# Building a scan's phase tables on GpSimd, and one rotation of eight PSUM banks for an FFN

## The chip, the core and the metric

One core of a Trainium2 chip runs the whole program. The metric is device time in microseconds (us) from launch to end. The engines are TensorE (PE; its weight loads are shown apart as PEld), VectorE (DVE), ScalarE (ACT), GpSimd (POOL) and SyncE (SP), which here only issues DMAs. Each engine works through its own queue in order and waits on semaphores for the others.

## The reference, cut to what matters

One layer of a diffusion backbone over 2048 latent tokens with 1024 channels and 256 context tokens, in float32:

```
n      = modulate(rmsnorm(x))                      # latent and context
q,k,v,u,gates = split(n @ w_in)
a      = neighbourhood_attention(rope(q), rope(k), v, context keys, bias)
s      = s5_branch(u)      # per group and state p: h[t] = lam[p]*h[t-1] + B u[t], lam complex,
                           # forward and backward, y = Re(C h) + D u, gelu, GLU
h      = x + g1 * ((sig(ga)*(a@w_ba) + sig(gs)*(s@w_bs)) @ w_out)
f      = modulate(rmsnorm(h))
h      = h + g2 * ((silu(f@W1) * (f@W2)) @ w_ffn_out)       # hidden 2816
out    = rmsnorm(h) * g
```

## The kernel before

Every matmul operand is split into a rounded high part and a remainder (`split`, L68: ACT writes `whi`, L70, then DVE writes `wlo`, L71), and each product is three matmuls. Weights come through SP's DMAs in pieces (`raw`, `piece`) and pass two short buffer rotations, `wr` (raw) and `wh` (split pairs; four pairs in the FFN).

A scheduling compiler orders the instructions of each engine. It goes by the order of the program, by priorities set in the code and by its own estimate of each instruction's time. `hot()` raises the priority of a few instructions, above all evacuations of PSUM. `run` (L1203) gives the scan and then the attention the high priority. The input projection (`in_proj`) stands 100000 lower and fills what they leave free, and the merge another 100000 lower.

**The scan** (`s5`, L629). Tokens are taken in chunks of 8, so that the scan runs over 288 chunk columns (32 of context, 256 latent). Eight sub-blocks are made (four `q`, two `sb` each), and each has two pairs of groups and two directions, so 32 rounds in all (L729 to L773). A round needs a table of the phases exp(i*theta*t) for 288 columns, real part `er` and imaginary part `ei`. It is built by doubling: 32 columns are copied from `eb`, then four levels (m = 32, 64, 128, 256; widths 32, 64, 128, 32) each multiply what is there by a complex constant from `zz`. ACT makes the copies (L734, L735) and one product of each part (L741, L742), DVE the two others with the sums (L743, L744). Then PE makes `pv` (L750), DVE rotates it with the table (L757 to L760), runs the scan instruction (L762), rotates back (L765, L766) and writes the states `hs` (L771, L772). `er` and `ei` have two buffers, `ea` and `eb` one. POOL issues the loads of `ut` (L651) for the scan. In the same stretch it builds the attention's bias tables (`biases`, L430): for each of 8 heads a load (L436), four additions (L442, L443) and three stores (L445), through the same ring of 12 buffers from which `in_proj` takes its `n` tiles.

While scan and projection run, only two PSUM banks (pool `gpm`) belong to the projection. Its evacuations are by DVE (L384 and what follows) and ACT (L382, L412, L426).

**The FFN** (`ffn`, L1096) goes through four blocks of 512 tokens; each has three groups of hidden tiles. For every hidden tile pair `ffn_in` (L1019) is called twice. It is one step of a fast 2x2 block multiplication: seven products (`prod`, L1063) of 12 matmuls with 256 columns (L1067 to L1069), in place of eight. Its weight sums are made by POOL (L1036 to L1050), and four pieces are split in the order s13, s24, (a11, a22), a12. The products share two PSUM banks, each as two halves: `pa` and `pb`.

| product, in order | writes | read by |
|---|---|---|
| s1 | pb half 1 | ACT copy to v, L1076 |
| s3 | pb half 0 | DVE add into v, L1079 |
| s2 | pa half 1 | DVE add into u, L1085 |
| s4 | adds to pb half 1 | DVE, L1087 |
| a11 | pa half 0 | ACT copy to u, L1084 |
| a22 | adds to pb half 0 | DVE, L1090 |
| a12 | adds to pa half 0 | ACT copy, L1093 |

Within one bank a write by PE and a read by another engine are kept apart by semaphores, also where the halves differ. The tiles `ps` come from a pool of four banks, so two calls fit. Behind a group's calls the output product runs (L92 to L94 with `po`): for both halves `c` of the channels, four token tiles each hold one bank of another pool of four (`fpo`) through all hidden tiles of the group, and are then added to `acc`. In a block's last group the next block's normalized input `X` is prepared between the weight pieces (`norm_ffn`, L990), in four steps that take two `ps` banks each.

Of the kernel before, what the change touches and what calls it, by code (L numbers as in the profile page):

```python
# [10 lines left out]
F32 = mybir.dt.float32  # L11
F32R = mybir.dt.float32r
BF16 = mybir.dt.bfloat16
AF = mybir.ActivationFunctionType
ALU = mybir.AluOpType
PSUM = bass.MemoryType.PSUM
DRAM = bass.MemoryType.DRAM

P = 128
# [33 lines left out]
class Kernel:  # L53
# [575 lines left out]
    def s5(self):  # L629
        nc, I = self.nc, self.I  # L630
        V = nc.vector
        with ExitStack() as ctx:
# [7 lines left out]
            for q in range(4):  # L640
                yn = [bp.tile([P, SC, 8, 16], F32, name=f"yn{cb}") for cb in range(2)]
                for sb in range(4 // NQ):
# [84 lines left out]
                    for p0 in range(0, NQ, 2):  # L727
                        hst = {}
                        for p in (p0, p0 + 1):  # L729
                            for d in range(2):  # L730
                                pr = d * 16 + pr0 + p
                                er = pp.tile([P, SEQC], F32, name="er")
                                ei = pp.tile([P, SEQC], F32, name="ei")
                                nc.scalar.copy(er[:, 0:32], self.eb[:, 0, :, pr])  # L734
                                nc.scalar.copy(ei[:, 0:32], self.eb[:, 1, :, pr])  # L735
                                for i, m in enumerate((32, 64, 128, 256)):
                                    w = min(m, SEQC - m)
                                    zr, zi, zn = (self.zz[:, i, x, pr:pr + 1] for x in range(3))
                                    ea = pp.tile([P, P], F32, name="ea", bufs=1)
                                    eb = pp.tile([P, P], F32, name="eb", bufs=1)  # L740
                                    nc.scalar.activation(ea[:, :w], er[:, 0:w], AF.Copy, scale=zr)  # L741
                                    nc.scalar.activation(eb[:, :w], ei[:, 0:w], AF.Copy, scale=zr)  # L742
                                    V.scalar_tensor_tensor(er[:, m:m + w], ei[:, 0:w], zn, ea[:, :w], op0=ALU.mult, op1=ALU.add)  # L743
                                    V.scalar_tensor_tensor(ei[:, m:m + w], er[:, 0:w], zi, eb[:, :w], op0=ALU.mult, op1=ALU.add)  # L744
# [274 lines left out]
    def ffn_in(self, ch, b, X, pm, os, tp, up):  # L1019
# [40 lines left out]
        pa = pm.tile([P, 2, 256], F32, name="ps")  # L1060
        pb = pm.tile([P, 2, 256], F32, name="ps")

        def prod(dst, a, x, first=True):  # L1063
            for k in range(4):
                mm = nc.tensor.matmul
                xh, xl = X[k][:, 0, x], X[k][:, 1, x]
                mm(dst, a[0][:, k], xh, start=(first and k == 0), stop=False, skip_group_check=True)  # L1067
                mm(dst, a[0][:, k], xl, start=False, stop=False, skip_group_check=True)  # L1068
                mm(dst, a[1][:, k], xh, start=False, stop=(k == 3), skip_group_check=True)  # L1069
# [4 lines left out]
        prod(pb[:, 1], s1, 3)  # L1074
        with self.hot():
            nc.scalar.copy(v, pb[:, 1])  # L1076
        prod(pb[:, 0], s3, 5, False)
        with self.hot():
            V.tensor_tensor(v, pb[:, 0], v, op=ALU.add)  # L1079
        prod(pa[:, 1], s2, 4)  # L1080
        prod(pb[:, 1], s4, 2, False)
        prod(pa[:, 0], a11, 0, False)
        with self.hot():
            nc.scalar.copy(u, pa[:, 0])  # L1084
            V.tensor_tensor(u, pa[:, 1], u, op=ALU.add)  # L1085
            V.tensor_tensor(c[1][:, 1], u, v, op=ALU.add)
            V.tensor_tensor(c[0][:, 1], pb[:, 1], u, op=ALU.add)  # L1087
        prod(pb[:, 0], a22, 6, False)
        with self.hot():
            V.tensor_tensor(c[1][:, 0], pb[:, 0], u, op=ALU.add)  # L1090
        prod(pa[:, 0], a12, 1, False)
        with self.hot():
            nc.scalar.copy(c[0][:, 0], pa[:, 0])  # L1093
        return [x.rearrange("p a t -> p (a t)") for x in c]

    def ffn(self, xs_, os, xp, tp, pm, first):  # L1096
        nc, I = self.nc, self.I
        V = nc.vector
        with ExitStack() as ctx:
# [5 lines left out]
            up = self.pool("fu", 2, ctx)  # L1105
# [3 lines left out]
            po = self.pool("fpo", 4, ctx, space=PSUM)  # L1109
# [3 lines left out]
            for b in range(NB):  # L1113
# [4 lines left out]
                for g, (p0, p1) in enumerate(groups):  # L1118
# [45 lines left out]
                    for c in range(2):  # L1164
                        cs = slice(c * 512, c * 512 + 512)
                        pos = {j: po.tile([P, 512], F32, name="po") for j in range(4)}
# [178 lines left out]
```

## Time and profile before

| | us |
|---|---|
| median of 3 runs | 3296.73 |
| lowest and highest run | 3295.64, 3303.11 |
| the profiled execution's own time | 3294.7 |
| its span, first to last instruction | 3292.9 |
| PE busy | 3140.3 (95%) |
| PEld busy | 2738.5 (83%) |
| DVE busy | 2313.2 (70%) |
| ACT busy | 1598.6 (49%) |
| POOL busy | 882.4 (27%) |

All views are of one profiled execution. Busy time counts instructions at work. A matmul is shown longer than the distance to the next one, since matmuls are pipelined, so a busy PE is not a PE at its peak. A wait of an engine is shown with the instruction that ended it. The mean granted clock of TensorE was 0.983 of full speed.

### The profile page before, as it was taken

The numbers are of one execution on the slowest core, as the hardware profiler recorded it, in microseconds if no ns is written. First come the engines' busy times: TensorE is split into PE (matmuls) and PEld (weight loads), VectorE is DVE, ScalarE is ACT, GpSimd is POOL, SyncE is SP. The second block draws the span as 40 slices with busy tenths as digits, with TensorE's granted clock in tenths as the row PEclk, the third lists the DMA queues.
The fourth block names the chain that finished last, engine by engine and source line by source line (L and its number), as shares of the span: only waits on it lengthen the run. The fifth ranks groups of instructions, "written<-read, shape, count | busy, mean of one in ns | idle before, by whom it ended". The sixth has DMA issues, their size and how long they took to land.

```text
span 3292.9 us, 54200 instructions
## 1 busy us (share of the span) xinstructions
PE 3140.3 (95%) x20600; PEld 2738.5 (83%) x20600; DVE 2313.2 (70%) x4121; ACT 1598.6 (49%) x2778; POOL 882.4 (27%) x856
## 2 busy tenths in 40 slices
PE   8999978999899999899999999999999999999998
PEld 6987766777788778778898888889989898989988
DVE  6688787888353475565657766887869856886666
ACT  4455434554465545456553444444535543554534
POOL 2000052001232222223200444632241423442242
PEclk9999989999999999999999999999999999999999
DMA  8445566445776887786847334434344333343332
GB/s 333 171 122 168 170 203 221 164 140 165 231 210 189 243 267 231 225 261 191 259 145 243 131 129 137 138 128 144 113 139 146 121 116 130 134 149 130 107 112 100
DMA packets 212852, 564.27 MB, mean 171 GB/s; under 512 B 31784, under 2 KB 63656, under 8 KB 212592
## 3 DMA queue, kind: packets, MB, share of 16 engines
q1 hardware_dynamic: 155008, 437.48, 40.1%
q0 software_dynamic: 28032, 87.64, 9.8%
q10 hardware_dynamic: 29552, 35.70, 3.2%
q8 instruction: 162, 2.65, 0.3%
q14 instruction: 98, 0.80, 0.1%
HBM read 446.95 MB, written 111.61 MB: 170 GB/s over the span
## 4 chain that ended last, share of the span: by engine, by line
PE 72%; DVE 11%; DMA 9%; issue 3%; ACT 2%; POOL 2%; SPq 0%; ACTq 0%; DVEq 0%; POOLq 0%
PE ps L92 10%; PE ps L94 10%; PE ps L93 10%; PE ps L1067 6%; PE ps L1069 6%; PE ps L1068 6%; PE po L93 4%; PE po L92 4%; PE po L94 4%; DVE wlo L71 4%; PE o L924 3%; DMA raw<-in_w_m 2%; DMA n<-in_rpb 2%; PE w L884 2%; PE w L905 1%
## 5 line engine op out<-in xcount | busy, mean ns | idle before, releaser
L71 DVE TENSOR_TENSOR wlo<-raw,whi 128x1024 fp32r<-128x1024 f32 (+1 forms) x522 | 661.5, 1269 | 350.1 <-ACT whi L70 341.3
L70 ACT CAST whi<-raw 128x1024 fp32r<-128x1024 f32 (+1 forms) x522 | 507.6, 974 | 536.0 <-PE ps L1068 141.5
L1067 PE MATMUL ps<-X,whi 128*128 128x256 f32 x2464 | 700.0, 285 | 30.8 <-DVE u L1085 10.6
L1069 PE MATMUL ps<-X,wlo 128*128 128x256 f32 x2464 | 689.9, 285 | 10.0 <-DVE wlo L71 8.6
L1068 PE MATMUL ps<-X,whi 128*128 128x256 f32 x2464 | 694.4, 283 | 0.0
L1067 PEld LDWEIGHTS ps<-X,whi 128*128 128x128 f32 x2464 | 471.7, 191 | 42.2 <-DVE u L1085 16.2
L1069 PEld LDWEIGHTS ps<-X,wlo 128*128 128x128 f32 x2464 | 465.8, 191 | 17.9 <-DVE wlo L71 17.9
L1068 PEld LDWEIGHTS ps<-X,whi 128*128 128x128 f32 x2464 | 471.8, 191 | 1.3
L92 PE MATMUL ps<-n,whi 128*128 128x512 f32 (+1 forms) x800 | 321.5, 402 | 32.0 <-DVE t L384 17.6
L93 PE MATMUL ps<-n,whi 128*128 128x512 f32 (+1 forms) x800 | 318.4, 398 | 0.0
L94 PE MATMUL ps<-n,wlo 128*128 128x512 f32 (+1 forms) x800 | 317.5, 398 | 0.0
L93 PE MATMUL po<-wlo,zh 128*128 128x512 f32 x704 | 277.6, 394 | 0.0
L94 PE MATMUL po<-whi,zl 128*128 128x512 f32 x704 | 275.6, 394 | 0.0
L92 PE MATMUL po<-whi,zh 128*128 128x512 f32 x704 | 270.4, 394 | 0.0
L92 PEld LDWEIGHTS ps<-n,whi 128*128 128x128 f32 x800 | 152.6, 191 | 73.0 <-DVE t L384 14.7
L1049 POOL TENSOR_TENSOR os<-raw 128x512 f32<-128x512 f32 x66 | 96.2, 1457 | 391.6 <-DMA raw<-in_w_f 364.2
L1050 POOL TENSOR_TENSOR os<-raw,os 128x512 f32<-128x512 f32 x88 | 147.0, 1670 | 190.4 <-DMA raw<-in_w_f 188.2
L71 DVE TENSOR_TENSOR wlo<-os,whi 128x1024 fp32r<-128x1024 f32 x110 | 149.2, 1356 | 60.8 <-ACT whi L70 60.6
L70 ACT CAST whi<-os 128x1024 fp32r<-128x1024 f32 x110 | 115.3, 1048 | 143.8 <-POOL os L1050 41.9
L94 PEld LDWEIGHTS ps<-n,wlo 128*128 128x128 f32 x800 | 152.7, 191 | 36.3 <-issue 3.5
L93 PEld LDWEIGHTS ps<-n,whi 128*128 128x128 f32 x800 | 153.1, 191 | 33.7 <-issue 2.1
L92 PE MATMUL ps<-y,whi 128*128 128x512 f32 x384 | 157.1, 410 | 10.4 <-DVE t L968 5.1
(341 smaller groups left out, 7101.7 us busy)
## 6 DMA issues: line engine op xcount, KB each, us to landing
raw<-in_w_f SPq DMA_DIRECT2D x198, 512.0 KB
raw<-sums SPq DMA_DIRECT2D x66, 512.0 KB
raw<-in_w_gate SPq DMA_DIRECT2D x64, 512.0 KB
raw<-in_w_f SPq DMA_DIRECT2D x66, 256.0 KB
raw<-in_w_qk SPq DMA_DIRECT2D x32, 512.0 KB
gsc<-e ACTq DMA_DIRECT2D x64, 256.0 KB
raw<-in_w_m SPq DMA_DIRECT2D x32, 512.0 KB
t<-gsc SPq DMA_DIRECT2D x64, 256.0 KB
```

Of the source, the lines that this page charges most:

```text
L70: self.nc.scalar.copy(hi, x)
L71: self.nc.vector.tensor_tensor(lo, x, hi.bitcast(F32), op=ALU.subtract)
L92: mm(ps, l[0], r[0], start=first, stop=False)
L93: mm(ps, l[0], r[1], start=False, stop=False)
L94: mm(ps, l[1], r[0], start=False, stop=last)
L884: nc.tensor.matmul(slv, q[:, qs], kl, start=(n == 0), stop=(n == 1))
L924: nc.tensor.matmul(o[h, g, :, hf, :], l, r, start=(n == 0), stop=(n == nb + 1), skip_group_check=True)
L1049: nc.gpsimd.tensor_tensor(s24[:, 0], s13[:, 0], a11, op=ALU.subtract)
L1050: nc.gpsimd.tensor_tensor(s24[:, 1], a12, s24[:, 0], op=ALU.subtract)
L1067: mm(dst, a[0][:, k], xh, start=(first and k == 0), stop=False, skip_group_check=True)
L1068: mm(dst, a[0][:, k], xl, start=False, stop=False, skip_group_check=True)
L1069: mm(dst, a[1][:, k], xh, start=False, stop=(k == 3), skip_group_check=True)
```

## The change

In the scan, the real and the imaginary part of a table stand in one tile `ee` with two halves, and POOL alone builds it. One copy takes both parts of the first 32 columns. Each level is four instructions: both parts by the real constant, both parts by the imaginary constant into `ea`, then a subtraction for the real part and an addition for the imaginary part. A round thus has 17 POOL instructions in place of 10 on ACT and 8 on DVE. `er`/`ei` keep two buffers and `ea` one; `eb` falls away.

In the FFN, each call of `ffn_in` takes four banks and uses one half of each. The order of the products becomes s1, s3, a11, s2, s4, a22, a12, and `u` gets a third buffer. The pool `fpo` joins the `ps` pool in one rotation of eight banks, which also serves the output product and `norm_ffn`.

```
-  er = pp.tile([P, SEQC], F32, name="er")
-  ei = pp.tile([P, SEQC], F32, name="ei")
-  nc.scalar.copy(er[:, 0:32], self.eb[:, 0, :, pr])
-  nc.scalar.copy(ei[:, 0:32], self.eb[:, 1, :, pr])
+  ee = pp.tile([P, 2, SEQC], F32, name="er")
+  er, ei = ee[:, 0], ee[:, 1]
+  G = nc.gpsimd
+  G.tensor_copy(ee[:, :, 0:32], self.eb[:, :, :, pr])
   for i, m in enumerate((32, 64, 128, 256)):
       w = min(m, SEQC - m)
-      zr, zi, zn = (self.zz[:, i, x, pr:pr + 1] for x in range(3))
-      ea = pp.tile([P, P], F32, name="ea", bufs=1)
-      eb = pp.tile([P, P], F32, name="eb", bufs=1)
-      nc.scalar.activation(ea[:, :w], er[:, 0:w], AF.Copy, scale=zr)
-      nc.scalar.activation(eb[:, :w], ei[:, 0:w], AF.Copy, scale=zr)
-      V.scalar_tensor_tensor(er[:, m:m + w], ei[:, 0:w], zn, ea[:, :w], op0=ALU.mult, op1=ALU.add)
-      V.scalar_tensor_tensor(ei[:, m:m + w], er[:, 0:w], zi, eb[:, :w], op0=ALU.mult, op1=ALU.add)
+      zr, zi = (self.zz[:, i, x, pr:pr + 1].unsqueeze(1).to_broadcast([P, 2, w]) for x in range(2))
+      ea = pp.tile([P, 2, P], F32, name="ea", bufs=1)
+      G.tensor_tensor(ee[:, :, m:m + w], ee[:, :, 0:w], zr, op=ALU.mult)
+      G.tensor_tensor(ea[:, :, :w], ee[:, :, 0:w], zi, op=ALU.mult)
+      G.tensor_tensor(er[:, m:m + w], er[:, m:m + w], ea[:, 1, :w], op=ALU.subtract)
+      G.tensor_tensor(ei[:, m:m + w], ei[:, m:m + w], ea[:, 0, :w], op=ALU.add)
...
-  pa = pm.tile([P, 2, 256], F32, name="ps")
-  pb = pm.tile([P, 2, 256], F32, name="ps")
+  pb1, pb0, pa1, pa0 = (pm.tile([P, 2, 256], F32, name="ps")[:, 0] for _ in range(4))
...
-  prod(pb[:, 1], s1, 3)
+  prod(pb1, s1, 3)
   with self.hot():
-      nc.scalar.copy(v, pb[:, 1])
-  prod(pb[:, 0], s3, 5, False)
+      nc.scalar.copy(v, pb1)
+  prod(pb0, s3, 5)
   with self.hot():
-      V.tensor_tensor(v, pb[:, 0], v, op=ALU.add)
-  prod(pa[:, 1], s2, 4)
-  prod(pb[:, 1], s4, 2, False)
-  prod(pa[:, 0], a11, 0, False)
+      V.tensor_tensor(v, pb0, v, op=ALU.add)
+  prod(pa0, a11, 0)
   with self.hot():
-      nc.scalar.copy(u, pa[:, 0])
-      V.tensor_tensor(u, pa[:, 1], u, op=ALU.add)
+      nc.scalar.copy(u, pa0)
+  prod(pa1, s2, 4)
+  with self.hot():
+      V.tensor_tensor(u, pa1, u, op=ALU.add)
       V.tensor_tensor(c[1][:, 1], u, v, op=ALU.add)
-      V.tensor_tensor(c[0][:, 1], pb[:, 1], u, op=ALU.add)
-  prod(pb[:, 0], a22, 6, False)
+  prod(pb1, s4, 2, False)
   with self.hot():
-      V.tensor_tensor(c[1][:, 0], pb[:, 0], u, op=ALU.add)
-  prod(pa[:, 0], a12, 1, False)
+      V.tensor_tensor(c[0][:, 1], pb1, u, op=ALU.add)
+  prod(pb0, a22, 6, False)
   with self.hot():
-      nc.scalar.copy(c[0][:, 0], pa[:, 0])
+      V.tensor_tensor(c[1][:, 0], pb0, u, op=ALU.add)
+  prod(pa0, a12, 1, False)
+  with self.hot():
+      nc.scalar.copy(c[0][:, 0], pa0)
...
-  up = self.pool("fu", 2, ctx)
+  up = self.pool("fu", 3, ctx)
-  po = self.pool("fpo", 4, ctx, space=PSUM)
+  pm = Rotation(pm, 4, self.pool("fpo", 4, ctx, space=PSUM), 4)
-  pos = {j: po.tile([P, 512], F32, name="po") for j in range(4)}
+  pos = {j: pm.tile([P, 2, 256], F32, name="ps").rearrange("p a t -> p (a t)") for j in range(4)}
```

## Rows read from the trace of the kernel before

**Rows 1.** Busy time in stretches: scan, its bias part, FFN; us of each engine, clock, DMA.
```profile
165.00:825.00 660.00, 618.41 (x3432) 494.68 (x3431) 547.94 (x1113) 320.69 (x678) 89.33 (x104) 0.97 0.54 169
400.00:545.00 145.00, 112.97 (x615) 92.23 (x614) 115.70 (x189) 62.44 (x122) 63.03 (x66) 0.89 0.67 213
...
1822.00:3293.00 1471.00, 1421.87 (x9682) 1310.16 (x9681) 1095.19 (x1408) 689.12 (x1052) 541.34 (x355) 0.99 0.38 128
```

**Rows 2.** Waits of PE in the whole span: us in total, times, longest us.
```profile
PE ps L92 <- DVE t L384: 18.8, 8, 6.4
...
PE ps L92 <- ACT e L412: 10.9, 1, 10.9
PE ps L1067 <- DVE u L1085: 10.6, 11, 3.2
PE ps L1067 <- DVE u L1079: 10.5, 11, 1.6
...
PE ps L1069 <- DVE wlo L71: 8.6, 13, 1.9
...
PE ps L1067 <- ACT u L1076: 3.8, 2, 2.1
...
PE ps L1067 <- DVE n L1087: 2.8, 3, 1.6
```

**Rows 3.** Timeline of PE in the FFN: start us, us, engine, line, idle before.
```profile
2109.40 0.28 PE L1069 MATMUL ps<-X,wlo 128*128 128x256 f32 x1
2110.93 0.39 PE L1067 MATMUL ps<-X,whi 128*128 128x256 f32 x1 [1.25 <-DVE u L1079]
...
2577.09 0.39 PE L1067 MATMUL ps<-X,whi 128*128 128x256 f32 x1 [2.06 <-ACT u L1076]
2577.32 0.28 PE L1068 MATMUL ps<-X,whi 128*128 128x256 f32 x1
2577.43 0.29 PE L1069 MATMUL ps<-X,wlo 128*128 128x256 f32 x1
```

**Rows 4.** Timeline of DVE in the first of those two stretches.
```profile
2108.77 1.77 DVE L71 TENSOR_TENSOR wlo<-raw,whi 128x512 fp32r<-128x512 f32 x1
2110.47 0.41 DVE L1079 TENSOR_TENSOR u<-ps,u 128x256 f32<-128x256 f32 x1
```

**Rows 5.** The chain that ended last, 2095 to 2122 us (FFN, first block), by line.
```profile
by line: DVE wlo L71 20.8%; DVE n L1129 18.1%; PE ps L1067 13.0%; PE ps L1068 11.0%; PE ps L1069 10.4%; issue 7.8%; DVE n L1126 5.1%; DVE zl L71 4.5%; DVE n L1090 4.0%; ACT whi L70 3.9%; DVE u L1079 2.5%; DVE u L1085 1.3%; ACTq L70 0.1%; DV
```

**Rows 6.** Groups by line, the table's instructions: count, busy us, mean ns, idle before.
```profile
L741 ACT ACTIVATE ea<-er,zz 128x32 f32<-128x32 f32 (+2 forms) x128 | 44.2, 345 | 62.8 <-DVE er L743 61.7 <-DVE ei L744 0.4 <-issue 0.3
...
L742 ACT ACTIVATE eb<-ei,zz 128x32 f32<-128x32 f32 (+2 forms) x128 | 43.5, 340 | 26.9 <-DVE ei L744 21.0 <-DMA ks<-qt 2.8 <-DMA vs<-e 2.6
...
L743 DVE SCALAR_TENSOR_TENSOR er<-ei,zz,ea 128x32 f32<-128x32 f32 (+2 forms) x128 | 38.0, 297 | 3.4 <-ACT ea L741 2.5
...
L744 DVE SCALAR_TENSOR_TENSOR ei<-er,zz,eb 128x32 f32<-128x32 f32 (+2 forms) x128 | 37.7, 294 | 2.9 <-ACT eb L742 2.7
```

**Rows 7.** Timeline of DVE through scan rounds of one sub-block.
```profile
359.62 0.76 DVE L757 TENSOR_TENSOR p<-pv,er 128x576 f32<-128x576 f32 x1 [0.79 <-PE pv L750]
...
363.86 0.68 DVE L766 TENSOR_TENSOR p<-v,ei 128x512 f32<-128x512 f32 x1
...
365.89 0.42 DVE L772 TENSOR_TENSOR h<-p,p 64x256 f32<-64x256 f32 x1
...
377.13 0.76 DVE L757 TENSOR_TENSOR p<-pv,er 128x576 f32<-128x576 f32 x1
```

**Rows 8.** Groups by line on POOL, each shape apart; columns as in rows 6.
```profile
L442 POOL TENSOR_TENSOR n<-am,n 128x480 f32<-128x480 f32 x16 | 20.5, 1302 | 69.1 <-DMA n<-in_rpb 54.2 <-issue 14.9
L443 POOL TENSOR_TENSOR n<-n,am 128x480 f32<-128x480 f32 x16 | 18.6, 1168 | 0.2
...
L140 POOL MEMSET mhalf<- 128x4 f32 x1 | 0.1, 98 | 0.0
```

**Rows 9.** Waits of POOL in 165 to 825 us; columns as in rows 2.
```profile
POOL n L442 <- DMA n<-in_rpb: 54.2, 7, 10.0
```

**Rows 10.** Groups by line on DVE, 165 to 405 us (POOL nearly idle).
```profile
L71 DVE TENSOR_TENSOR wlo<-raw,whi 128x1024 fp32r<-128x1024 f32 x28 | 34.1, 1217 | 12.1 <-ACT whi L70 11.9
```

**Rows 11.** The same, 405 to 525 us (POOL at the bias tables).
```profile
L71 DVE TENSOR_TENSOR wlo<-raw,whi 128x1024 fp32r<-128x1024 f32 x12 | 17.2, 1431 | 5.2 <-ACT whi L70 5.2
```

## The prediction

> **What bounds the kernel now.** I read the page's engine shares first, then busy time by stretch, then who PE waited for, then timelines where those waits lie. PE is busy 95% of the span in the table of times. By stretch it is 618 of 660 us in the scan (0.97 of its clock) and 1422 of 1471 us in the FFN, where the next engine, DVE, has 1095; in the scan DVE has 548 of 660, ACT 321 and POOL 89 [rows 1]. So the time is PE's work plus PE's waits. The change leaves the matmuls as they are, so its worth is PE waits that go or come. DVE, ACT and POOL time counts only where it makes PE wait. The reader should see in [rows 2] that few waits are long enough to matter: for the scan stretch the projection's evacuation, L384 (18.8 us) and L412 (10.9); for the FFN the readers of the shared product banks and the weight split (8.6). And the weak spot in [rows 1]: in 400 to 545, where POOL makes the bias tables, PE has 113 of 145 us and a clock of 0.89.
>
> **FFN, what is removed.** Four rows of [rows 2] are PE waiting to write one half of a bank while the other half is read: L1085 10.6, L1079 10.5, L1076 3.8, L1087 2.8, together 27.7 us in 27 waits. A waiting matmul's predecessor is shown 0.28 us long although the next starts 0.11 to 0.12 us behind it where nothing waits (2577.32 to 2577.43) [rows 3], so each wait is understated by some 0.16 us: 27 x 0.16 = 4.3, in all 32.0 us. One of them, read closely: PE stands from 2109.40 to 2110.93 for L1079, which could not start before 2110.47 because a weight split of 1.77 us was ahead of it on DVE [rows 3, 4]. PE did not need that number; it needed the bank. With four banks per call, s3 no longer waits for the copy of s1, a22 no longer for the reads of s4's half, a12 no longer for L1085; s4 comes two products later and in a bank whose copy was taken four products before. All four waits lose their cause.
>
> **FFN, what comes back.** PE then runs on until something else is late, and next is the weight split, on the same DVE. In the first block DVE already sets the pace: in 2095 to 2122 wlo, L1129, L1126, zl and the evacuations L1090, L1079, L1085 make 56.3% of the chain, the matmuls 34.4% [rows 5]. The L1079 waits that I looked up lie mostly in that block, so I give back half of them, 5 us. The order is also less kind to weights: a11 is third instead of fifth, so its piece must be split two products earlier, while its buffer is still freed by the sixth product of the call before. And norm_ffn's eight bank requests now share the rotation with the output product: the third and fourth pair get banks that the first channel half holds until it has been added up. Eight is a whole turn, so the two calls of a pair still get different fours. For these two I give back 3 us; nothing, if the scheduler finds other products to put first, and up to 24 more if every removed wait turns into one for wlo. So the FFN gives 32 - 5 - 3 = **24 us**, bounds 0 and 32.
>
> **Scan, what is removed.** DVE loses L743 and L744, 38.0 + 37.7 = 75.7 us, and ACT L741 and L742, 44.2 + 43.5 = 87.7 us, and its copies [rows 6]. ACT is far from full there [rows 1], so its part is worth nothing by itself; the cover is PE's projection work.
>
> **Scan, what is added.** A table is 16 two-input instructions and a copy on POOL. Elements per partition: copy 64; products 2 x (64 + 128 + 256 + 64) = 1024; sums 2 x (32 + 64 + 128 + 32) = 512; in all 1600. The trace has no POOL instruction of these shapes. Nearest rows: L443, 480 elements with a broadcast operand, 1.17 us, and a memset of 4 elements, 0.098 us [rows 8]. If the time grows with the elements, that is 0.098 + 2.23 ns each, and a table costs 17 x 0.098 + 1600 x 0.00223 = 5.2 us. If every one cost a whole L443, 16 x 1.17 = 18.7 us. I take 5.2, since seven of ten elements are in instructions of 128 to 256 elements, between the two rows: 32 x 5.2 = 168 us of POOL, in a stretch where it had 89 of 660 [rows 1].
>
> Does the scan wait for it? A buffer is given back when L766 of two rounds before ends (364.5), and the round that uses it next starts L757 at 377.1, 12.6 us later; DVE's own work for a round runs from 359.6 to 366.3, 6.7 us [rows 7]. A POOL table of 5.2 us is inside both. So the rounds go no slower, rather a little faster, and PE's projection fills whatever they leave; of the L384 waits [rows 2] I take 3 us off, those outside the bias part being the smaller half.
>
> POOL and DVE disturb each other. The same weight split takes 1.217 us while POOL is nearly idle and 1.431 us, 18% more, while POOL makes bias tables [rows 10, 11]. POOL's additions there are 16 x 1.302 + 16 x 1.168 = 39.5 us of 120, 33% [rows 8]. At 168 us of about 645, 26%, I estimate 14% on DVE instructions. On the 472 us that DVE keeps in the scan (548 - 76) that is up to 66 us, which nearly eats the 75.7. Hence no more than the 3 us.
>
> The Trainium skill says the same in "SBUF — State Buffer", section "Who interferes with whom": a DVE instruction with two SBUF inputs contends with a GpSimd instruction that reads SBUF. The trace agrees with its 18%. The Trainium skill's "GPSIMD Engine Reference", section 4.1, advises against two-input elementwise work on GpSimd as about two times slower than on VectorE; no run so far has this table on POOL.
>
> **The bias part** is where POOL's order costs. L442 waits there 54.2 us in 7 waits for its load, 7.7 each, at most 10.0 [rows 9]; what stands behind it in POOL's queue waits too. Some four rounds fall in these 120 us. If their table instructions lie behind such a wait, L757 waits on DVE, behind it the projection's evacuations, and PE with its two banks. Bounds: nothing, if the tables fall into POOL's idle gaps; 4 x 7.7 = 31 us of waiting plus 4 x 5.2 = 21 us by which the bias chain is stretched, together 52. I take 7, near the lower end, since two tables are made ahead and a 5.2 us table fits a 7.7 us gap, which the scheduler may or may not use.
>
> **Sum**, on the profiled execution: 3294.7 - 24 (FFN) - 3 (scan rounds) + 7 (bias part) = 3274.7. That execution lies 2.0 us under the median of the runs, so the median should be 3276.7, **3277 us**, 0.6% faster. About 0.2%, 6.6 us, is what a measurement of this kernel can tell from no change.
>
> **Rivals.**
> - *The bias part holds up the scan* (the other side). One mechanism: tables queued on POOL behind L442's waits. For it: PE already loses 32 of 145 us there [rows 1], and POOL's queue is strictly in order. Against it: POOL idles between the heads. It gives +45 in place of +7: 3296.7 - 24 - 3 + 45 = 3315. It turns the sign beyond 27 + 6.6 = 34 us, four tables that each wait a whole load.
> - *The weight split takes over in the FFN.* For it: DVE's share of the chain [rows 5] and 8.6 us of wlo waits already there [rows 2]. Against it: the FFN's DVE is at 1095 of 1471 [rows 1]. The FFN gives 8: 3296.7 - 8 + 4 = 3293, no change to be told. If the joined rotation brought nothing else than new waits between the output product and the calls, it would look the same.
> - *POOL's tables are slow*, 18.7 us each with the slowing of DVE. Two buffers then give a table every (18.7 + 6.7) / 2 = 12.7 us, where the two rounds from 359.6 to 377.1 in [rows 7] took 8.8 each. 32 x 3.9 = 125 us later on DVE; PE has projection work for most of it, and I charge a fifth, 25: 3296.7 - 24 + 7 + 25 = 3305. This is what the Trainium skill's "GPSIMD Engine Reference", section 4.1, advises against.
> - *More than forecast.* All 32 us of the FFN come home and 15 of the 29.7 us of L384 and L412 [rows 2] go, because DVE and ACT answer sooner: 3296.7 - 32 - 15 = 3250.
>
> **How the numbers follow.** Chances: forecast 0.48, bias part 0.17, weight split 0.15, slow tables 0.08, more 0.12. The range reaches from the last case to the slow tables and part of the bias case: 3252 to 3306. That leaves about half of "more" below it and 0.1 above. The forecast's own range is 3266 to 3288. Faster by over 0.2%: 0.46 of the forecast, 0.12, a third of the weight case and a little of the bias case, 0.65. Within 0.2%: 0.02, half of the weight case and a fifth of the others, 0.14. Slower: the rest, 0.21.
>
> **What would show it.** PE's waits for L1079, L1085, L1076, L1087 (at their new lines) gone or under 5 us, and those for wlo not above 17: FFN right. POOL's table instructions of 0.17 to 0.67 us, 5 to 7 us a table, and L757 waiting for POOL hardly at all: scan right. L757 waiting on POOL for tens of us in the bias part, or PE busy under 105 us in its 145: the first rival. The prediction fails if the reordering by the scheduler moves loads or evacuations elsewhere, above all in the attention, which I count as unchanged.

## The result, and the profile after

| | before | after |
|---|---|---|
| median of 4 runs, us | 3296.8 | 3248.9 |
| lowest and highest run | 3295.6, 3303.1 | 3246.7, 3249.9 |
| span of the profiled execution | 3292.9 | 3247.2 |
| first product of the FFN starts (timeline of PE) | 1831.5 | 1817.7 |
| last matmul ends | 3284.6 | 3238.2 |

The ratio is 0.985, 95% interval 0.9833 to 0.9867: 48 us faster, outside the predicted range of 3252 to 3306 by 3 us and 28 us below the predicted value of 3277. From the last two rows, 13.8 us of it lie ahead of the FFN and 32.6 in the FFN (1453.1 to 1420.5).

Busy time by stretch, after; it answers to [rows 1]:

```profile
165.00:825.00 660.00, 627.23 (x3451) 498.09 (x3450) 540.35 (x851) 236.06 (x357) 381.24 (x641) 0.98 0.53 167
400.00:545.00 145.00, 125.82 (x673) 102.02 (x672) 109.01 (x147) 49.22 (x74) 91.90 (x123) 0.93 0.73 225
1822.00:3247.00 1425.00, 1391.62 (x9568) 1290.39 (x9566) 1101.87 (x1401) 677.75 (x1038) 545.49 (x350) 1.00 0.39 131
```

In the scan, POOL went from 89 to 381 us, ACT from 321 to 236. DVE lost table instructions that add up to 75.7 us [rows 6], but its busy time only fell from 548 to 540: much of what it kept got longer. In the bias part, where the prediction feared a loss, PE gained 13 us.

Waits of PE in the whole span, after; they answer to [rows 2]:

```profile
PE ps L92 <- DVE t L384: 13.6, 7, 5.1
PE w L904 <- ACT s L897: 12.4, 4, 6.7
PE ps L1067 <- DVE wlo L71: 11.3, 12, 1.7
PE pv L749 <- DVE p L757: 8.8, 2, 5.1
PE ps L1065 <- DVE u L1077: 7.7, 12, 1.6
...
PE ps L1065 <- ACT u L1080: 1.8, 1, 1.8
PE ps L1065 <- ACT u L1074: 0.8, 2, 0.4
```

The lines have moved: L1077 adds to v (L1079 before), L1080 copies u, L1074 copies v. The 10.9 us for L412 are gone, L384 fell from 18.8 to 13.6, and of the four bank waits only the addition to v keeps a size. New is pv waiting for L757: a DVE that is late in a round.

The FFN's 33 us don't all stand in a view of waits. I took, for each matmul there, the distance to the next start less the median distance for its kind, and added up those that lie over 60 ns:

| us (times) | before | after |
|---|---|---|
| ended by a reader of a product bank | 34.9 (39) | 13.0 (17) |
| ended by a weight split | 18.4 (40) | 17.1 (17) |
| no wait shown, some 0.1 us each | 18.3 (185) | 8.6 (87) |
| sum | 71.6 | 38.7 |

The third row is for the most part the waits again. Of the 185 before, 95 (10.5 us) follow a start that was itself late: the start behind a delayed one comes 0.1 us late too, as 2577.09, 2577.32, 2577.43 in [rows 3] show (0.23 us, then 0.11). Another 64 (6.0 us) lie in four stretches of 3.4 us in which TensorE was granted half of its clock, 1.2 GHz in place of 2.4. After, the two kinds are 37 (3.8 us) and 25 (2.5 us, in one stretch of 6.8 us). One such stretch before, with the 20 us ahead of it, in which PE waited 1.7 us for L1076 and 3.2 for L1085 (columns as in [rows 1]):

```profile
2200.00:2220.40 20.40, 15.46 (x92) 13.37 (x91) 16.18 (x20) 10.12 (x18) 13.23 (x11) 1.00 0.25 89
2220.40:2223.80 3.40, 3.40 (x19) 3.40 (x18) 3.40 (x4) 1.92 (x5) 3.40 (x5) 0.50 0.26 72
```

### The profile page after: what moved, and what is told of

Its sections match the earlier page's. It is cut to its first block, busy times and chain, and to the rows that moved or that the text cites. A ratio compares the mean times of both kernels' runs of the same rounds, so it can differ in the third digit from the quotient of the medians.

```text
span 3247.2 us, 54190 instructions
## 1 busy us (share of the span) xinstructions
PE 3124.2 (96%) x20600; PEld 2727.0 (84%) x20600; DVE 2321.7 (71%) x3865; ACT 1511.2 (47%) x2458; POOL 1193.5 (37%) x1400
## 4 chain that ended last, share of the span: by engine, by line
PE 74%; DVE 10%; DMA 9%; POOL 3%; issue 3%; ACT 1%; SPq 0%; DVEq 0%; POOLq 0%; ACTq 0%
PE ps L92 14%; PE ps L94 14%; PE ps L93 14%; PE ps L1067 7%; PE ps L1065 7%; PE ps L1066 7%; DVE wlo L71 3%; PE o L923 3%; DMA n<-in_rpb 2%; PE w L883 1%; DMA y<-as 1%; PE w L904 1%; DMA raw<-in_w_m 1%; PE pv L749 1%; DMA raw<-in_w_bs 1%
## 5 line engine op out<-in xcount | busy, mean ns | idle before, releaser
L71 DVE TENSOR_TENSOR wlo<-raw,whi 128x1024 fp32r<-128x1024 f32 (+1 forms) x522 | 696.9, 1342 | 332.3 <-ACT whi L70 322.7
L1067 PE MATMUL ps<-X,wlo 128*128 128x256 f32 x2464 | 692.6, 284 | 11.5 <-DVE wlo L71 11.3
L92 PE MATMUL ps<-n,whi 128*128 128x512 f32 (+1 forms) x800 | 319.5, 400 | 17.1 <-DVE t L384 11.2
L92 PE MATMUL ps<-whi,zh 128*128 128x512 f32 x704 | 277.1, 395 | 0.0
L94 PE MATMUL ps<-whi,zl 128*128 128x512 f32 x704 | 277.0, 394 | 0.0
L93 PE MATMUL ps<-wlo,zh 128*128 128x512 f32 x704 | 276.9, 394 | 0.0
L1048 POOL TENSOR_TENSOR os<-raw 128x512 f32<-128x512 f32 x66 | 118.1, 1789 | 402.6 <-DMA raw<-in_w_f 321.4
L70 ACT CAST whi<-os 128x1024 fp32r<-128x1024 f32 x110 | 115.4, 1049 | 204.6 <-PE ps L1066 91.8
L1049 POOL TENSOR_TENSOR os<-raw,os 128x512 f32<-128x512 f32 x88 | 132.9, 1510 | 154.3 <-DMA raw<-in_w_f 152.3
L93 PEld LDWEIGHTS ps<-n,whi 128*128 128x128 f32 x800 | 152.4, 190 | 34.9 <-issue 3.3
```

The source lines that it names most:

```text
L70: self.nc.scalar.copy(hi, x)
L71: self.nc.vector.tensor_tensor(lo, x, hi.bitcast(F32), op=ALU.subtract)
L92: mm(ps, l[0], r[0], start=first, stop=False)
L93: mm(ps, l[0], r[1], start=False, stop=False)
L94: mm(ps, l[1], r[0], start=False, stop=last)
L1048: nc.gpsimd.tensor_tensor(s24[:, 0], s13[:, 0], a11, op=ALU.subtract)
```

## The experiments

In the diffs a minus is the kernel before unless said otherwise. "Before" ran beside each group at medians of 3297.8 to 3300.8; the ratios take care of that.

**One half at a time.** e1_scan_only is the kernel before with the table on POOL alone, e2_ffn_only the kernel before with the whole FFN half alone.

> The scan half alone on the kernel before. Theory A (the scan half is worth its share of what the changed kernel gained ahead of the FFN, where the first FFN matmul came 13.8 us earlier, 1831.5 to 1817.7): 3297 - 14 = 3283 us, and the FFN stretch as long as before, 1461 us. Rival B (the forecast's term, +4, with the tables' 9.7 us each in place of 5.2 and VectorE relieved of nothing): 3297 to 3303 us; then the 14 us ahead of the FFN come from the other half. Both expect GpSimd busy near 1190 us and VectorE near 2315.

> The FFN half alone. Theory A: the FFN stretch shrinks by 32 us (1461 to 1429) and nothing ahead of it moves: 3297 - 32 = 3265 us, and the two halves add up to the whole 48. Rival B: this half brings all of it, 3297 - 48 = 3249, since the reordering reaches back into the merge. Rival C (the forecast): 24 us, 3273.

Measured: 3281.5, ratio 0.9953 (0.9937 to 0.997), 16 us faster; and 3265.9, ratio 0.9901 (0.9883 to 0.9919), 32 us faster. Together 48: the halves add up to the whole change. The prediction had 24 faster for the FFN half and 4 slower for the scan half.

**The FFN half, edit by edit.** e3_old_order has four banks, the joined rotation and the third u buffer, but the old order of products; e4_rotation_only has only the joined rotation.

```
 # e3_old_order, against the changed kernel
-prod(pa0, a11, 0); copy u; prod(pa1, s2, 4); add u; prod(pb1, s4, 2, False)
+prod(pa1, s2, 4); prod(pb1, s4, 2, False); prod(pa0, a11, 0); copy u; add u
 # e4_rotation_only, against the kernel before
-po = self.pool("fpo", 4, ctx, space=PSUM)
+pm = Rotation(pm, 4, self.pool("fpo", 4, ctx, space=PSUM), 4)
```

> The FFN half alone, four banks a call and eight in rotation, but the seven products in the old order (s1, s3, s2, s4, a11, a22, a12). If the separate banks do it, the order is worth little: within 4 us of the FFN half with the new order. If the forecast was right that a11 as third product costs weight waits, this is 3 us or more faster. If the new order is needed to give each read its time, this is 10 us or more slower.

> Only the rotation is joined; a call keeps two shared banks and the old order, so that four calls would find room. Theory A (the readers of the shared halves are the cause): the 27.7 us of waits for L1085, L1079, L1076 and L1087 stay, 3292 to 3298 us. Rival (room for more calls is what counts): those waits shrink to under 10 us and the time to under 3280.

Measured: e3 3287.0, ratio 0.9962 (0.9947 to 0.9977), 11 us; e4 3305.0, ratio 1.0022 (1.0012 to 1.0032), 7 us slower, above both of its ranges. In e4 the four bank waits stay, at 29.8 us (27.7 before), as its theory A said. Waits of PE in the FFN of e3:

```profile
PE ps L1066 <- ACT u L1083: 26.2, 28, 1.5
PE ps L1068 <- DVE wlo L71: 8.5, 12, 1.0
PE ps L1066 <- DVE u L1078: 6.1, 7, 1.4
```

L1083 copies u out of a11's bank. In the old order only a22 stands between a11 and a12, which adds to the same bank: 12 matmuls, and the copy is often later than that. In the kernel before, PE waits for L1085 instead, which comes behind that copy and reads the same bank; four banks without the new order leave the wait for the copy.

The remaining two corners: e9_order_alone has the new order with the old two shared banks, e8_two_fours has four banks and the new order, but the rotation taken apart.

```
 # e8_two_fours, against the changed kernel
-pm = Rotation(pm, 4, self.pool("fpo", 4, ctx, space=PSUM), 4)
+po = self.pool("fpo", 4, ctx, space=PSUM)      # and pos from po
 # e9_order_alone: as e8, and
-pb1, pb0, pa1, pa0 = (pm.tile(...)[:, 0] for _ in range(4))
+pa, pb = (pm.tile(...) for _ in range(2))      # two halves each
```

> The changed kernel with the joined rotation of eight taken apart: the seven products have their own four banks (all four in each call) and the output product its own four; the order of the products stays new. A call then gets the banks of the call before. Theory A (the new order alone keeps each bank's reader at least one product away, and eight are not needed): within 8 us of the changed kernel, 3249 to 3257. Theory C (the next call's first products wait for the last reads of the call before): each of 176 pairs of calls loses 0.1 us or more, 3265 to 3285.

> The changed kernel with the FFN's old banks and the new order: two shared banks a call from a pool of four, the output product in its own four, order s1, s3, a11, s2, s4, a22, a12. The scan half is in, so the reference point without the FFN half is 3281. Theory (four banks and the order need each other): a11 and s2 now stand side by side in one bank, so s2 waits for ACT's copy of a11 in nearly every one of 352 calls, some tens of us of waits, and s3 for the copy of s1: 3285 to 3320, no gain from the order alone. Rival (the order by itself is what helps): 3255 to 3270.

Measured: e8 3250.7, ratio 0.9857 (0.9839 to 0.9874), the changed kernel's time; e9 3325.5, ratio 1.0081 (1.0066 to 1.0096), 44 us above e1, past the upper end of both expectations. Waits of PE in the FFN of e9:

```profile
PE ps L1069 <- DVE wlo L71: 22.8, 24, 2.3
PE ps L1067 <- DVE u L1079: 22.1, 25, 2.0
PE ps L1067 <- ACT whi L70: 15.8, 13, 2.4
...
PE ps L1067 <- ACT u L1082: 0.9, 3, 0.3
```

The wait that I had named, s2 for the copy of a11 (L1082), is 0.9 us. What grew is the wait for v's addition (22.1) and for weights: 38.6 us for splits, against 14.0 after. So what the prediction charged for an earlier a11 may be what appears here, though only with shared banks. The joined rotation brings nothing: without it the time is the same (e8), and alone it costs 7 us (e4). Four banks a call together with the new order are what counts.

**What a table costs where it was.** Three kernels on the base of before. In e5_no_table all rounds read one constant table; e6_no_handover has that too, and all 18 instructions of a table stay on ACT and DVE, but read constants and write scratch; e7_pool_unread has the constant table, and POOL makes tables that nobody reads.

```
 # e6_no_handover
-nc.scalar.activation(ea[:, :w], er[:, 0:w], AF.Copy, scale=zr)
-V.scalar_tensor_tensor(er[:, m:m + w], ei[:, 0:w], zn, ea[:, :w], ...)
+nc.scalar.activation(da[:, :w], er[:, 0:w], AF.Copy, scale=zr)       # er, ei: constant
+V.scalar_tensor_tensor(dv[:, :w], ei[:, 0:w], zn, er[:, :w], ...)    # da, dv: unread
```

> The kernel before with no phase table made at all: one table of constants is written once and every round reads it (the output is then not the reference's). This is the worth of taking the table off ACT and DVE with nothing put in its place. Theory A (what counts is the hand-overs between ACT and DVE inside the table: in the kernel before ACT waits 61.7 us for L743, 21.0 for L744 and 12.9 for L765 between 165 and 825 us, with the projection's copies behind it in its queue): 3270 to 3280, some 20 us faster than before. Theory B (the recorded sum: nothing to be had there but a few us): 3290 to 3295. If it comes out near 3281, the time of the scan half alone, POOL's own table costs nothing; if it is far below, POOL's table costs the difference.

> The kernel before with the table's work left on ACT and DVE, instruction for instruction, but with no hand-over: ACT's ten instructions and DVE's eight read the constant table and write into scratch that nobody reads, so neither waits for the other (the output is then not the reference's). Theory A (hand-overs): at least two thirds of what the kernel with no table gains comes here too, 3275 to 3285. Theory B (the busy time: 75.7 us of DVE and some 105 of ACT): under a third, 3290 to 3300, since both engines are as busy as before.

> The kernel with no table, and beside it POOL making all 32 tables as in the changed kernel, into a tile that nobody reads (the output is then not the reference's). It has POOL's work and its disturbance of DVE, but no round waits for a table. If disturbance is what POOL's tables cost: the time of the scan half alone, 3279 to 3284, and above the kernel with no table. If the wait of the rounds for POOL (16.7 us in the changed kernel's DVE) is what they cost: equal to the kernel with no table within 3 us. If neither costs anything: all three equal.

Measured: e5 3261.0, ratio 0.9873 (0.9854 to 0.9891), 38 us faster; e6 3267.2, ratio 0.9902 (0.9887 to 0.9917), 32 us; e7 3301.0, ratio 1.0003 (0.9994 to 1.0013). Busy time in 165 to 825 us, e6:

```profile
165.00:825.00 660.00, 622.82 (x3474) 499.34 (x3473) 563.85 (x1120) 336.85 (x686) 103.59 (x119) 0.97 0.55 172
```

DVE and ACT are busier here than before (548 and 321), and the kernel is 32 us faster, so the table's work on the two engines is not what cost most. The hand-overs between their in-order queues went, and [rows 6] had shown them, in the last column: ACT stood 62.8 us ahead of L741 and 26.9 ahead of L742, mostly for DVE. But 32 of 38 us is not their share in the scan. Taken over 165 to 1000 us, the sums over PE's starts (table further below) give e5 19.4 us and e6 11.6, so some 60%. The rest of both, 15.3 and 19.5 us, lies in 1000 to 1800, in attention and merge. No edit touches an instruction there, but the scheduling compiler gave another order: of the 1043 DVE instructions of before, 1040 come in the same order in e2 and e4, 780 in e1 and 707 in e6. e7 shares 991 of its DVE instructions in that order with e5 (1012), and has the low sum there too, 69.3, although its scan lost 20 us. So that part goes with the new order, and not with what the scan gained.

What can stand behind a hand-over on ACT is seen at the longest PE wait of [rows 2], 10.9 us for L412. Timeline of ACT, before, and PE's wait:

```profile
442.74 0.62 ACT L652 COPY un<-ut 128x512 f32<-128x512 f32 x1 [13.16 <-DMA ut<-us]
...
449.41 0.25 ACT L734 COPY er<-eb 128x32 f32<-128x32 f32 x1 [3.31 <-DVE p L765]
449.69 0.32 ACT L741 ACTIVATE ea<-er,zz 128x32 f32<-128x32 f32 x1
449.92 0.57 ACT L412 COPY e<-ps 128x512 f32<-128x512 f32 x1
...
450.54 0.58 PE L92 MATMUL ps<-whi,n 128*128 128x256 f32 x1 [10.89 <-ACT e L412]
```

ACT first waited for a load, the first 3.1 us of PE's wait, then, after other copies and with the projection's bank long full, 3.31 us for a table buffer that DVE had not yet given back. Only then came L412, and PE. So the table's part of these 10.9 us is a third.

e7 did not isolate what it was built for: with nobody reading, POOL ran its tables far ahead, the loads of ut stood behind them (ACT waited 68.0 us for ut in 165 to 900) and PE had 208 of 235 us in 165 to 400, against 233 before.

**POOL's tables: disturbance, queue or wait?** x2_pool_ts takes the changed kernel's products with a per-partition scalar instead of a broadcast second tensor. x1_ut_sp and x5_ut_act move the loads of ut to SP and to ACT; x4_both and x6_ts_ut_act combine each with the lighter products.

```
 # x2_pool_ts, against the changed kernel
-G.tensor_tensor(ee[:, :, m:m + w], ee[:, :, 0:w], zr, op=ALU.mult)   # and ea with zi
+G.tensor_scalar(ee[:, :, m:m + w], ee[:, :, 0:w], zr, None, op0=ALU.mult)
 # x1_ut_sp; x5_ut_act with nc.scalar
-nc.gpsimd.dma_start(u0[:n]...)
+nc.sync.dma_start(u0[:n]...)
```

> The changed kernel with the loads of ut (24 of them) issued by SP in place of POOL, so that no load stands behind a table in POOL's queue. Theory D (the tables delay these loads: in the kernel that makes unread tables ahead of time ACT waited 68 us for ut and PE had only 208 of 235 us in 165 to 400, against 228 in the changed kernel and 233 before): PE gets back up to 6 us there, 3240 to 3246. Rival: SP's queue is in order too, and a ut load that waits for its buffer holds up the weight loads behind it: 3252 or more, with PE waiting for whi behind raw.

> The changed kernel with the two products of each level as instructions with a per-partition scalar in place of a broadcast second tensor: the same 17 instructions and the same numbers, 8 of them with one tensor to read in place of two. Theory E (POOL's table is 9.5 us instead of the 5.2 of the recorded sum because of the second operand and the disturbance from DVE; lighter products shorten the table and disturb DVE less): a table of 7 us or less, the mean scan instruction under 840 ns (885 in the changed kernel, 756 before), 3238 to 3246. Rival (a POOL instruction's time does not depend on it): same table, 3247 to 3252.

> Both edits together: ut loads by SP and products with a per-partition scalar. If the two theories hold, 3230 to 3242, below each alone; if SP's queue is the rival that holds, no better than the lighter products alone.

> The changed kernel with the loads of ut issued by ACT, which is also the engine that copies ut and so frees its buffer: no load waits behind a table, and none waits in a queue for another engine. If the place in POOL's queue costs: 3240 to 3246. If it doesn't: 3247 to 3253.

> Lighter products and ut loaded by ACT together: 3228 to 3236 if the queue costs, 3236 to 3242 if it doesn't.

Measured: x1 3267.3, ratio 0.9902 (0.9886 to 0.9918); x2 **3238.3**, ratio 0.9816 (0.9796 to 0.9835); x4 3247.8, ratio 0.9849 (0.9833 to 0.9866); x5 3269.6, ratio 0.9906 (0.9886 to 0.9927); x6 3266.6, ratio 0.9894 (0.9875 to 0.9914). The theory that moving the loads away from the tables would gain falls: each of the four kernels with the loads moved is slower than its partner, by 10 to 28 us, and on ACT too, so SP's queue can't be the whole reason. Why was not settled. x2 is the fastest kernel of the study, but not as expected: its table got longer, not shorter. Groups on POOL in 165 to 825 us, first after, then x2:

```profile
L741 POOL TENSOR_TENSOR ea<-er,zz 128x64 f32<-128x64 f32 x64 | 33.0, 516 | 2.6
L742 POOL TENSOR_TENSOR er<-er,ea 128x32 f32<-128x32 f32 x64 | 28.6, 447 | 2.8
...
L740 POOL TENSOR_TENSOR er<-er,zz 128x256 f32<-128x256 f32 x32 | 25.5, 797 | 2.3
```

```profile
L741 POOL TENSOR_SCALAR ea<-er,zz 128x64 f32<-128x64 f32 x60 | 42.8, 713 | 3.0
L740 POOL TENSOR_SCALAR er<-er,zz 128x256 f32<-128x256 f32 x30 | 41.3, 1377 | 2.8
```

It waits more for POOL, too (DVE at L756: 29.9 us, after 16.7), and its mean scan instruction takes 806 ns against 885.

The paced pair was made to separate disturbance from waiting. The rounds read a table that is there; POOL makes another in each round, started by a one-column copy on DVE.

```
 # e10_paced (e11_paced_ts: the same with tensor_scalar products)
+er, ei = (self.eb[:, x]... for x in range(2))     # rounds read this
+V.tensor_copy(ee[:, 0, 0:1], pv[:, 0, 0:1])       # then POOL's 17 instructions into ee, unread
```

> The kernel before, the rounds reading a table that is there from the start (a stretch of the persistent tile eb, so the output is not the reference's), and POOL making a table of its own in each round that nobody reads. A one-column copy from pv on DVE starts it, so that POOL can't run ahead. It has POOL's disturbance of DVE and its place in POOL's queue, but no round waits for a table. If the disturbance (and the queue) eat the 22 us between no table (3261) and POOL's table (3281): 3275 to 3284, with the mean scan instruction at 850 to 890 ns. If the rounds' waits for their table eat them: 3261 to 3268.

> The same with the products as instructions with a per-partition scalar. If disturbance by the second operand is the price: 5 to 12 us below the paced kernel with broadcast products, the scan instruction near 810 ns. If not: equal to it within 3 us.

Measured: e10 3308.8, ratio 1.003 (1.0019 to 1.0042); e11 3278.7, ratio 0.9935 (0.9917 to 0.9953). e10 fits neither expectation: without any wait for the table it is 27 us slower than e1, whose rounds do wait. So it does not price the disturbance. The same sums over PE's starts as in the FFN table, here of all late starts, show where such differences lie:

| us | before | e1 | e5 | e6 | e7 | after | x2 | e10 | x5 |
|---|---|---|---|---|---|---|---|---|---|
| 165 to 1000 | 95.2 | 87.8 | 75.8 | 83.6 | 115.1 | 84.0 | 88.6 | 94.5 | 94.2 |
| 1000 to 1800 | 87.5 | 74.4 | 72.2 | 68.0 | 69.3 | 82.0 | 63.2 | 96.2 | 90.1 |

Each column is one execution. Four kernels have the order of before ahead of the FFN (before, e2, e3, e4): 95.2 to 100.5 in the first stretch, 84.2 to 87.5 in the second. Four others share the order of the changed kernel (e1, after, e8, e9): 84.0 to 89.1 and 74.4 to 82.0. So a difference of 5 us or more in one row can be chance, and in the means the scan half gained 12 us in the scan stretch and 8 in attention and merge.

Of the 28 us between e1 and e10, 22 stand behind 1000 us, and so does all that x2 has over the changed kernel: in attention and merge, where no variant's edit changes an instruction. Hence the last pair: the changed kernel and x2 with work that should not count, to see what another order from the scheduling compiler does.

```
+G.memset(ea[:, 0, 0:1], 0.0)      # in each level, overwritten right after
```

> The changed kernel with one memset of one column on POOL in each level of a table, 128 in all, some 13 us of POOL in a stretch where it idles 280 of 660 us, overwritten right after. If only real work moves the time: 3248 to 3252. If the order that the compiler chooses is worth as much as the variants tried: anywhere in 3235 to 3275, with the difference spread over 1000 to 1800 us too.

> The kernel with lighter products (3238) with the same memsets. If the lighter products are why it beat the changed kernel: 3236 to 3243 and below the run beside it by about 10. If that was the order: anywhere in 3232 to 3265, and above or below the run beside it.

Measured: e12 3249.0, ratio 0.9857 (0.9831 to 0.9883), no change; e13 3244.9, ratio 0.9831 (0.9816 to 0.9847), 7 us above x2, with intervals that overlap. The order did change, in e12 in the attention (763 of 1049 DVE instructions come as in after), in e13 mostly in the scan (909 of 1010 as in x2). So a new order alone moved the time by 0 and at most some 7 us here; whether it can bring the 15 to 20 us that e5 and e6 have behind 1000 us, these two don't show. In all five pairs (after and x2, e12 and e13, x1 and x4, x5 and x6, e10 and e11) the lighter products are faster, by 11, 4, 19, 3 and 30 us; for 4 and 3 the intervals overlap. The sign is likely, the size is not known, and that disturbance is its cause was argued from the scan instruction's mean, not shown.

## Why the prediction was wrong, point by point

The direction and the place of the FFN's gain were right. Two terms of the sum failed, 8 us in the FFN and 20 in the scan, and one premise: that the attention stays as it was.

**FFN, 24 forecast, 32 measured (e2).** "All four waits lose their cause" held for three; the addition to v keeps 7.7 us, above the bound of 5 that the prediction gave, so what came back was charged to the right wait. By the starts of the matmuls, bank readers cost 34.9 us where the forecast had worked out 32.0, and 21.9 of them went, with 1.3 of the splits: 23, close to the 24. The failed step is the price of a wait. The forecast added 0.16 us to each, and the start behind it, 0.1 us late as well, and the stretches at half clock were left out; those late starts went from 18.3 to 8.6 us, the missing 9.7. The charge of 3 us for weights and rotation did not come: waits for wlo went from 8.6 to 11.3, under the prediction's bound of 17, but by the starts splits cost 17.1 against 18.4. Four banks without the order bring 11, the order without four banks costs 44, both bring 32.

**Scan, +4 forecast, -16 measured (e1).** The step that failed: "ACT is far from full there, so its part is worth nothing by itself". The busy share was read, the idle time in the same rows was not: ACT stood 90 us at L741 and L742, most of it for DVE, in an in-order queue with evacuations behind. In 165 to 825 us PE's waits for L384 and L412 fell from 28.9 to 7.4 us (e1 6.0), and with the table's work left on both engines but without hand-overs (e6) to 10.7. New waits took part of that back, so the scan stretch gained 12 us where the sum lost 4. The prediction also named what would undo it, a reordering "above all in the attention, which I count as unchanged": attention and merge were reordered and gained some 8 us, with no cause shown. The rival "more than forecast" had the right rows: over the whole span L384 and L412 together fell from 29.7 to 13.6, 16 us where it said 15. That its 3250 is within 1 us of the result is in part luck, since it knew neither the new waits nor the attention; its chance was 0.12, and the range ended at 3252, above it.

**The price of a table** was forecast as 5.2 us, between 5.2 and 18.7. All groups of the table on POOL after add up to 305 us, 9.5 each. The line from elements to time was not far off: where DVE stands idle, a table's instructions add up to 6.1 us (two to nine cases of each form). Two of them while DVE waited for this table (until 476.41, below), 290 and 630 ns where the line gives 241 and 669:

```profile
472.88 0.63 POOL L740 TENSOR_TENSOR er<-er,zz 128x256 f32<-128x256 f32 x1
475.75 0.29 POOL L741 TENSOR_TENSOR ea<-er,zz 128x64 f32<-128x64 f32 x1
```

Over all rounds the same two forms take 797 and 516 ns. "POOL and DVE disturb each other" was charged to DVE alone; POOL's own side of it, 3.4 us a table, was left out. (The prediction's "seven of ten elements" are 1024 of 1600, 64%.)

**DVE's relief** was forecast to be nearly eaten, up to 66 us of 75.7, 14% on each instruction. Added up by instruction, DVE's work in 165 to 825 us without the table was 538.4 us before and is 580.7 after: 42 us more, 8%. (Busy times can't be set against the 75.7: one instruction often starts before the one ahead of it ends, as in [rows 4], and busy time counts the overlap once.) So the mechanism was right and its size was overrated. Which instructions pay most is visible; the four groups shown make 16 of the 42 us. Groups on DVE in 165 to 825 us, before:

```profile
L762 DVE TENSOR_TENSOR_SCAN v<-r,v 128x288 f32<-128x288 f32 x64 | 47.2, 756 | 0.0
L757 DVE TENSOR_TENSOR p<-pv,er 128x576 f32<-128x576 f32 x32 | 24.1, 752 | 7.3 <-PE pv L750 7.1
L766 DVE TENSOR_TENSOR p<-v,ei 128x512 f32<-128x512 f32 x32 | 22.6, 706 | 0.0
L760 DVE TENSOR_TENSOR v<-p,p 128x288 f32<-128x288 f32 x32 | 14.4, 449 | 0.0
```

and the same four after:

```profile
L761 DVE TENSOR_TENSOR_SCAN v<-r,v 128x288 f32<-128x288 f32 x64 | 54.4, 885 | 0.0
L765 DVE TENSOR_TENSOR p<-v,er 128x512 f32<-128x512 f32 x32 | 25.7, 804 | 0.0
L756 DVE TENSOR_TENSOR p<-pv,er 128x576 f32<-128x576 f32 x32 | 24.2, 755 | 24.0 <-POOL er L742 16.7 <-PE pv L749 5.3
L759 DVE TENSOR_TENSOR v<-p,p 128x288 f32<-128x288 f32 x32 | 20.3, 634 | 0.0
```

The rotation that reads pv from PSUM is unchanged (752, 755 ns); the three that read two tiles in SBUF take 14%, 17% and 41% more. The Trainium skill says this in "SBUF — State Buffer", section "Who interferes with whom": a DVE instruction with two SBUF inputs contends with a GpSimd instruction that reads SBUF. The four rows agree, the unchanged one included.

**The bias part**, +7 forecast, with 45 as a rival. The mechanism exists. DVE at its longest wait, after, and POOL's queue ahead of it:

```profile
476.41 0.76 DVE L756 TENSOR_TENSOR p<-pv,er 128x576 f32<-128x576 f32 x1 [12.32 <-POOL er L742]
```

```profile
458.94 0.54 POOL L740 TENSOR_TENSOR er<-er,zz 128x64 f32<-128x64 f32 x2
459.43 0.75 POOL L445 DMA_DIRECT2D bi<-n  x1
465.86 2.39 POOL L442 TENSOR_TENSOR n<-am,n 128x480 f32<-128x480 f32 x2 [5.68 <-DMA n<-in_rpb]
468.21 0.32 POOL L742 TENSOR_TENSOR er<-er,ea 128x64 f32<-128x64 f32 x1
```

A half-made table stands behind L442, which waits for its load, and behind more of the bias work after it. It happens twice, 12.3 and 4.4 us, not four times, and PE's bias stretch gained 13 us all the same: the 10.9 us for L412, which lay there, are gone. The rival that followed the Trainium skill's "GPSIMD Engine Reference", section 4.1 (two-input elementwise work is better left to VectorE), 3305, did not come: each instruction is slower, as that section says (a first level's product takes 516 ns on POOL for the 64 elements of both parts, where DVE took 260 for product and sum of one part's 32), but the kernel is faster; in the scan stretch the crossing between two queues seems to have cost more than the work (e6, 11.6 of 19.4 us).

**What stays open.** No table at all gives 38 us and POOL's table 16; which part of the other 22 is disturbance, waiting or order is not settled, since e7 and e10 brought effects of their own. Every edit of the scan also reordered the attention, and no run holds that order fixed: the 8 us of the change there, and 15 to 20 of e5 and e6, have no cause shown. Why moving the loads of ut costs 10 to 28 us is not known. A third buffer for er was not tried.

## What to carry to other kernels

Read the idle time ahead of an engine's instructions, not only its busy share: a chain that passes between two in-order queues level by level charges its waits to everything queued behind it, and moving it whole to a third, slower engine can pay, as the 12 us of the scan stretch here. Give each accumulating product its own bank together with an order that puts other products between a write and the next write to the same bank; here one product between was too few (28 waits, 26 us) and three were enough for most, and either edit alone gave a third of the gain or a loss. Price a wait with what follows it: the start behind it was 0.1 us late too. When a scheduling compiler sits between the edit and the chip, run a neutral edit as well, compare the order in the stages that the edit doesn't touch, and add up start-to-start distances by stage: more than half of what seemed to be the worth of the hand-overs (19.5 of 31 us in e6) lay in a stage that was reordered, but not edited.

## What the runs showed of the hardware that I had not expected

POOL's product with a per-partition scalar is slower than the one with a broadcast tensor (713 against 516 ns for 64 elements, 1377 against 797 for 256; the shortest of the 64, 435 against 284). The slowing between POOL and DVE goes both ways: a table takes POOL 6.1 us where DVE is idle and 9.5 on average beside it. On DVE it is uneven: 41% for a 288-column sum of two SBUF tiles, nothing for a 576-element product that reads PSUM.
